# Output projection of a gated encoder layer as 2x2 block products: seven multiplications for eight, with the weight sums kept in DRAM

## The chip, the core and the metric

The kernel runs on one core of a Trainium2 chip. The core has TensorE (PE, matmuls, with its weight loads listed as PEld), VectorE (DVE), ScalarE (ACT), GpSimd (POOL) and SyncE (SP, which here only issues DMAs). SBUF is the working memory, PSUM takes the results of matmuls. The metric is the device time of one execution in microseconds.

## The reference

One encoder layer is applied to a prompt of 1024 tokens and a sample of 512 tokens, with the same weights. Three branches (pooling, self-attention, cross-attention) are projected to 1024 channels, gated and added; then comes the output projection that is changed here, a norm and the residual:

```
merged = jnp.zeros_like(x)
for n in range(N_BRANCH):
    merged = merged + gates[:, :, n] * (branches[n] @ w_branch[n])
y = rms_norm(merged @ w_out, ln_post)
return x + y
```

`w_out` is 1024 x 1024. Everything is float32.

## The kernel before

Each float32 matmul is done as three faster ones: an operand x is split into a high part (a copy rounded to the matmul's input type, made on ACT, L167) and a low part (x minus the high part, on DVE, L164), and `mm3` (L134) adds high x high, high x low and low x high in PSUM.

**Weights.** `weights` (L176) loads one tile of 128 x 1024 from DRAM into one of three raw buffers and splits it into `whi` and `wlo`. These have two buffers each (`NW`), so the split of a tile waits until PE is done with the tile before the last. Loads are issued by SP in its order. A raw buffer is free again when the low part is made.

**Input projection.** `products` (L323) already works on 2x2 blocks with seven products for the prompt's two token blocks. Beside it, small pieces of other work (`background`, L464) are run from a list `tasks`: the tails of keys, queries and pooling. One piece is taken at each product.

**Branches and merge.** The prompt is worked in two blocks of 512 tokens. `branches` (L1001) runs over three branches in the order 0, 2, 1 and over eight channel chunks d of 128. `merge` (L1051) multiplies one chunk; one weight tile serves two chunks, 24 matmuls of 512 columns. DVE applies the gate (L1064) and POOL adds to the accumulator (L1066). The accumulator is two tiles, `acc[0]` for channel chunks 0 to 3 and `acc[1]` for 4 to 7, each 128 x (4 x 512 tokens). In the last branch every second chunk is followed by a split of the two finished chunks (`split_pair`).

**Output projection.** `out_phase` (L1073) takes the split chunks as stationary operands, 128 tokens at a time, and the tiles of `w_out` as moving ones, in two column halves of 512. Each half runs over four weight tiles; a tile holds two chunks and serves 4 token tiles x 2 chunks x 3 = 24 matmuls. `evacuate` (L1093) reads each finished PSUM bank twice: DVE multiplies by the norm's row (`lnpost`) into `y`, ACT sums the squares. `finish` (L1081) makes the root mean square for two token tiles at a time (a sum on DVE, two small operations on POOL) and then scales and adds the residual on DVE (L1090), with low priority in the order. For the sample (`last`) there is a different ending.

The order of the instructions on each engine is made ahead of time by a scheduler from the code's order and the priorities (`AHEAD` for weight splits, `EVAC` for evacuations). On the chip each engine works through its own list in that order and waits for semaphores.

Of the kernel before, what the change touches and what calls it, by code (L numbers as in the profile page):

```python
# [14 lines left out]
AF = mybir.ActivationFunctionType  # L15
# [4 lines left out]
P = 128  # L20
D = 1024
# [41 lines left out]
def encoder_kernel(ctx: ExitStack, tc, wt, xs, xts, mt, cols, rows, rope, edge, ys):  # L63
# [112 lines left out]
    def weights(*key, pieces=1):  # L176

        raw = RAW()
        load(raw[:], wt[TILES[key]])
# [266 lines left out]
    def group(g):  # L446
# [53 lines left out]
        def gate_to_scratch(m, c0):  # L500
            def take(i, j, b, s):
                x = summed(b, s)
                o = HU()[:, :n] if s is None else s
# [144 lines left out]
    def pool_tail(c, ut, gate, T, out, wide, two_wide):  # L648
# [26 lines left out]
        for b in range(T // BLK):  # L675
# [324 lines left out]

    def branches(b, sc, merged):  # L1001

# [19 lines left out]
        def rest():  # L1022
            for i, (n, d) in enumerate(steps):
# [4 lines left out]
                if 2 <= d < 6 and n != order[-1]:  # L1028
                    chunk(order[order.index(n) + 1], d - 2)
                yield from merge(n, d, gates.pop(i), br, acc, merged if n == order[-1] else None)  # L1030

# [9 lines left out]
    def block(g, b, sc, last, merged=None):  # L1041
        bs = slice(b * BLK, (b + 1) * BLK)
        if merged is None:
            merged = []
            first, rest = branches(b, sc, merged)
            for f in first:
                f()
            yield from rest
        yield from out_phase(merged, xs[g][bs, :], ys[g][bs, :], last)

    def merge(n, d, sg, br, acc, merged):  # L1051

# [12 lines left out]
        if n > 0:  # L1065
            pool.tensor_tensor(at, at, sg, op=ALU.add)  # L1066
        if merged is not None and d % 2:
            merged.extend(split_pair(acc[d // 4][:, (d % 4 - 1) * BLK:(d % 4 + 1) * BLK]))
        yield

    held = []

    def out_phase(merged, src, dst, last):  # L1073
        y = [M(F32) for _ in range(2)]
# [6 lines left out]
        def finish(i):  # L1081
            ss = S(2)
            v.reduce_sum(ss[:], ssq[:, 2 * i:2 * i + 2, :2], axis=AX.X)
            rstd_of(ss[:])
            with tc.high_priority(-LATER):
                for j in range(2):
                    t = 2 * i + j
                    x = U()
                    load(x, src[t * P:(t + 1) * P, :])
                    v.scalar_tensor_tensor(x, yv[i][:, j], ss[:, j:j + 1], x, op0=ALU.mult, op1=ALU.add)  # L1090
                    nc.sync.dma_start(dst[t * P:(t + 1) * P, :], x)

# [5 lines left out]

        for half in range(1 if last else 2):
            o = [B(), B()] if half else [a[:, i * BLK:(i + 1) * BLK] for a in (A(),) for i in range(2)]  # L1100
            o += [a[:, i * BLK:(i + 1) * BLK] for a in (A(),) for i in range(2)]
            n = slice(half * BLK, half * BLK + BLK)
            for c in range(4):
                w = weights("half", half, c)
                for pair in ((0, 1), (2, 3)):
                    for kk in range(2):
                        k, s = c * 2 + kk, slice(kk * BLK, kk * BLK + BLK)
                        for t in pair:
                            ts = slice(t * P, (t + 1) * P)
                            mm3(o[t][:], (merged[k][0][:, ts], merged[k][1][:, ts]), w(s), k == 0, k == KC - 1)  # L1110
                    if c == 3:
                        for t in pair:
                            evacuate(t, n, o[t][:], half)
                    yield
        if last:
            av = A()[:].rearrange("p (t n) -> p t n", t=TT)
            for c in range(2):
                w = weights("out", 0, c)
                for kk in range(4):
                    k, s = c * 4 + kk, slice(kk * 256, kk * 256 + 256)  # L1120
                    for t in range(TT):
                        ts = slice(t * P, (t + 1) * P)
                        mm3(av[:, t], (merged[k][0][:, ts], merged[k][1][:, ts]), w(s),
                            k == 0 and t % 2 == 0, k == KC - 1 and t % 2 == 1)
                    yield
            for t in range(TT):
                evacuate(t, slice(512, 768), av[:, t], 1)
            yield from ending(merged, src, dst, yv, ssq, lnpost)
            return
        for i in range(2):  # L1130
            finish(i)

# [48 lines left out]
    bare = False  # L1181
    first, rest = branches(0, sc, merged)
    fill = chain(led(fill, len(pairs[1]) * 4, first), rest)
# [103 lines left out]
```

## Time and profile before

| | us |
|---|---|
| three runs | 1460.95, 1459.49, 1457.48 (median 1459.49) |
| the profiled execution | 1458.94 |
| its span, first to last instruction | 1456.7 |

One profile is taken of one execution. The parts read here are the page (busy times, and the span in 40 slices), the busy time of each engine by stretch, the groups of instructions, the chain of waits that ended last, and the timeline (start, duration, engine, line, output<-inputs, shape, and in brackets the idle time before it with what ended it). In a timeline row "x2" stands for two instructions in a row, with the time from the start of the first to the end of the second. Rows of an engine that follow each other closely overlap by some 0.1 us, so the distance of their starts is what one costs in a queue.

The stretches of the prompt's end are: branches of block 0 until 1187 us, its output projection until 1230, the branches of block 1 until 1296, its projection until 1340, then the sample.

### The profile page before, as it was taken

To read this page: it belongs to the slowest core of one execution; us is meant where nothing else is said; L and a number is where in the kernel's file an instruction comes from. 1 tells how busy PE (TensorE), PEld (TensorE's weight loads), DVE (VectorE), ACT (ScalarE), POOL (GpSimd) and SP (SyncE) were. 2 spreads that over 40 slices of the span, in tenths; PEclk is the share of its full clock that TensorE was granted. 3 is DMA by queue.
4 is the path that set the end of the run, shared out by engine and by line. 5 is a ranking of instruction groups with operands and counts; after the bars stand their busy time and mean duration, and the time that the engine had idled before them with its cause. 6 is when DMAs were issued, how large, how long until landed. Compare 5 with 4: busy or idle time off the path is not lost. (4 is left out here: it accounts for less than half of the span.)

```text
span 1456.7 us, 19518 instructions
## 1 busy us (share of the span) xinstructions
PE 1429.7 (98%) x7264; PEld 1198.0 (82%) x7264; DVE 969.6 (67%) x1211; ACT 712.1 (49%) x1085; POOL 276.0 (19%) x286
## 2 busy tenths in 40 slices
PE   6999999999999999999999999999999999999998
PEld 5878888888888888788888888888888888888887
DVE  6896586666557674565777666677676665765764
ACT  6454444544434545443666666677675233234232
POOL 1000020110000000210223322333333230240231
PEclk9999999999999999999999999999999999999999
DMA  8312243331422443244655665565447745945842
GB/s 288 118 64 98 80 131 115 114 132 61 132 93 69 153 145 123 87 163 148 240 204 192 222 216 189 209 209 172 148 159 266 270 127 180 333 166 184 329 137 86
DMA packets 95375, 238.65 MB, mean 164 GB/s; under 512 B 10672, under 2 KB 18992, under 8 KB 95280
## 3 DMA queue, kind: packets, MB, share of 16 engines
q1 hardware_dynamic: 86064, 203.84, 42.0%
q10 hardware_dynamic: 9216, 33.56, 5.9%
q8 instruction: 57, 0.93, 0.3%
q14 instruction: 38, 0.31, 0.1%
HBM read 151.38 MB, written 52.43 MB: 140 GB/s over the span
## 5 line engine op out<-in xcount | busy, mean ns | idle before, releaser
L128 PE MATMUL B<-med,whi 128*128 128x512 f32 x1576 | 492.0, 392 | 3.1 <-ACT med L440 1.3
L128 PE MATMUL A<-med,whi 128*128 128x512 f32 x1200 | 373.6, 392 | 1.4 <-ACT med L167 1.0
L128 PEld LDWEIGHTS B<-med,whi 128*128 128x128 f32 x1576 | 291.4, 188 | 62.7 <-ACT med L440 1.5
L167 ACT ACTIVATE whi<-raw 128x1024 fp32r<-128x1024 f32 (+1 forms) x169 | 167.4, 991 | 296.3 <-PE A L128 148.2
L128 PE MATMUL B<-med,wlo 128*128 128x512 f32 x788 | 308.0, 391 | 0.0
L164 DVE TENSOR_TENSOR wlo<-raw,whi 128x1024 fp32r<-128x1024 f32 (+1 forms) x169 | 212.1, 1255 | 139.3 <-ACT whi L167 137.7
L128 PEld LDWEIGHTS A<-med,whi 128*128 128x128 f32 x1200 | 223.1, 188 | 47.9 <-ACT med L167 1.2
L128 PE MATMUL A<-med,wlo 128*128 128x512 f32 x600 | 234.1, 390 | 0.1
L128 PEld LDWEIGHTS B<-med,wlo 128*128 128x128 f32 x788 | 147.9, 188 | 31.1
L189 POOL TENSOR_SCALAR s<-s 128x16 f32<-128x16 f32 (+3 forms) x17 | 7.5, 444 | 663.0 <-DVE s L582 324.0
L128 PEld LDWEIGHTS A<-med,wlo 128*128 128x128 f32 x600 | 112.6, 188 | 24.6 <-DVE wlo L164 0.8
L164 DVE TENSOR_TENSOR med<-A,med 128x1024 fp32r<-128x1024 f32 (+1 forms) x93 | 112.8, 1214 | 28.2 <-ACT med L167 26.6
L167 ACT ACTIVATE med<-A 128x1024 fp32r<-128x1024 f32 x92 | 94.2, 1025 | 68.5 <-PE A L132 68.1
L807 POOL TENSOR_SCALAR u<-u,s 128x1024 f32<-128x1024 f32 x64 | 72.3, 1129 | 212.3 <-DVE s L806 174.5
L803 DVE TENSOR_REDUCE s<-A 128x1 f32<-128x1024 f32 x64 | 77.8, 1215 | 36.8 <-PE A L128 31.8
L1066 POOL TENSOR_TENSOR med<-med,med 128x512 f32<-128x512 f32 x48 | 76.0, 1594 | 127.9 <-DVE med L1064 90.6
L128 PE MATMUL A<-whi,med 128*128 128x512 f32 (+1 forms) x352 | 98.3, 360 | 0.0
L805 ACT ACTIVATE u<-A,s 128x1024 f32<-128x1024 f32 x64 | 71.4, 1115 | 40.6 <-issue 23.4
L128 PE MATMUL A<-kt,med 128*128 128x512 f32 x320 | 87.8, 395 | 0.0
L167 ACT ACTIVATE whi<-sum 128x1024 fp32r<-128x1024 f32 x50 | 52.9, 1061 | 61.2 <-PE B L128 37.2
L164 DVE TENSOR_TENSOR med<-med,med 128x1024 fp32r<-128x1024 f32 (+1 forms) x50 | 55.6, 1120 | 32.7 <-ACT med L167 28.7
L164 DVE TENSOR_TENSOR wlo<-sum,whi 128x1024 fp32r<-128x1024 f32 x50 | 61.0, 1221 | 22.7 <-ACT whi L167 21.6
(197 smaller groups left out, 1899.3 us busy)
## 6 DMA issues: line engine op xcount, KB each, us to landing
raw<-wt SPq DMA_DIRECT2D x168, 512.0 KB, 3.7
u<-u ACTq DMA_DIRECT2D x64, 512.0 KB, 3.1
merge<-hu SPq DMA_DIRECT2D x72, 256.0 KB, 2.1
med<-merge SPq DMA_DIRECT2D x72, 256.0 KB, 5.7
med<-br SPq DMA_DIRECT2D x36, 256.0 KB, 5.3
q<-hu SPq DMA_DIRECT2D x24, 256.0 KB, 2.4
br<-hu SPq DMA_DIRECT2D x24, 256.0 KB, 2.8
med<-q SPq DMA_DIRECT2D x12, 512.0 KB, 4.8
```

Of the source, the lines that this page charges most:

```text
L128: pe.matmul(out, l, r, **k)
L164: v.tensor_tensor(out, x, hi.bitcast(F32), op=ALU.subtract)
L167: act.activation(hi, x, AF.Copy)
L189: pool.tensor_scalar(ss, ss, EPS, 1.0, op0=ALU.add, op1=ALU.mult)
L803: v.reduce_max(mx[:], a[:], axis=AX.X, negate=True)
L805: act.activation(p, a[:], AF.Exp, bias=mx[:], accum_out=sm[:])
L807: pool.tensor_scalar(p, p, rc[:], 1.0, op0=ALU.mult, op1=ALU.mult)
L1066: pool.tensor_tensor(at, at, sg, op=ALU.add)
```

## The change

The projection of a block becomes a product of 2x2 blocks: the tokens in two halves of 256, the channels in two halves of 512, the columns in two halves of 512. With quarters a11 to a22 of the merged block (`quarter`) and b11 to b22 of the weights, seven products are made in this order: a11 b11; a12 b21; s2 w2; s3 w3; s4 w4; s5 b22; a22 w6, where s3 = a21 + a22, s2 = s3 - a11, s4 = a11 - a21, s5 = a12 - s2. Each product has two weight tiles of 12 matmuls. The products are added up in three pairs of PSUM banks (X, Y, Z); three intermediate results are copied to SBUF by ACT (`keep`), and `put` adds them on DVE, takes the squares on ACT from SBUF, and multiplies by the norm's row on POOL.

The weight sums w2, w3, w4, w6 are made once by `out_weights`, a background task that is put on the list in the second pair of the first merge gate's projections, and are written to DRAM (`wsum`). Later they are loaded like any weight tile. The sample's projection is as before.

```diff
+    wsum = {i: scratch(f"wsum_{i}", [P, 2 * D]) for i in (2, 3, 4, 6)}
+    def out_weights():
+        for c in range(2):
+            b11, b12, b21, b22 = [U() for _ in range(4)]
+            for x, half, k in ((b11, 0, 0), (b12, 1, 0), (b21, 0, 2), (b22, 1, 2)):
+                load(x, wt[TILES["half", half, k + c]])
+            for _ in range(4):
+                yield
+            v.tensor_tensor(b12, b22, b12, op=ALU.subtract)
+            v.tensor_tensor(b11, b12, b11, op=ALU.add)
+            yield
+            v.tensor_tensor(b22, b22, b11, op=ALU.subtract)
+            v.tensor_tensor(b21, b21, b11, op=ALU.subtract)
+            yield
+            for i, x in ((4, b12), (2, b11), (3, b22), (6, b21)):
+                nc.sync.dma_start(wsum[i][:, c * D:(c + 1) * D], x)
+            yield
...
-        if merged is not None and d % 2:
-            merged.extend(split_pair(acc[d // 4][:, (d % 4 - 1) * BLK:(d % 4 + 1) * BLK]))
+        if parts:
+            parts(d, acc, merged)
...
+    def by_quarters(d, acc, merged):
+        if d == 3:
+            merged.append(quarter_parts(quarter(acc, 0, 0)))
+        elif d == 7:
+            merged.append([quarter(acc, i, j) for i in range(2) for j in range(2)])
...
+    def out_products(merged, src, dst):
...
+        def left(i):
+            if i == 1:
+                return quarter_parts(a12)
+            if i == 2:
+                total(3, a21, a22, ALU.add)
+                total(2, sums[3], a11, ALU.subtract)
+            elif i == 4:
+                total(4, a11, a21, ALU.subtract)
+            elif i == 5:
+                total(5, a12, sums[2], ALU.subtract)
+            return quarter_parts(a22 if i == 6 else sums[i])
...
+        def put(t, n, b, k):
+            ns = slice(n * BLK, (n + 1) * BLK)
+            x, junk = yv[t // 2][:, t % 2, ns], HU()
+            with tc.high_priority(EVAC):
+                if k is None:
+                    act.activation(x, b, AF.Copy)
+                else:
+                    v.tensor_tensor(x, b, kept.pop(k)[:], op=ALU.add)
+                act.activation(junk[:], x, AF.Square, scale=0.25 * D ** -0.5, accum_out=ssq[:, t, n:n + 1])
+            pool.tensor_tensor(x, x, lnpost[:, ns], op=ALU.mult)
...
+        for i in range(7):
+            lhs, bank = ahead, "XYXZXZX"[i]
...
+            for c in range(2):
+                w = right(i, c)
+                if c == 0 and i < 6:
+                    ahead = left(i + 1)
...
+                        mm3(b[u], (lhs[0][:, 2 * c + k, us], lhs[1][:, 2 * c + k, us]), w(ks),
+                            i in (0, 1, 3) and c == k == 0, c == k == 1, skip_group_check=True)
```

What stands in the lists of the engines is shown at two places. The first is VectorE's list in the first block's projection. Names are tile and instruction number; `wlo` is the low part of a weight tile, `med` from `med` or `u` the low part of a quarter or sum, `u` from two tiles a sum of quarters. Before, from the last weight tiles of the first column half on, with the two evacuations of L1096 between them:

```order
L164 TENSOR_TENSOR wlo_10840<-raw_10837,whi_10839 128x1024
L164 TENSOR_TENSOR wlo_10870<-raw_10867,whi_10869 128x1024
L164 TENSOR_TENSOR wlo_10915<-raw_10912,whi_10914 128x1024
L1096 TENSOR_TENSOR med_10769<-A_10775,u_10772 128x512 x2
L1096 TENSOR_TENSOR med_10770<-A_10776,u_10772 128x512
L164 TENSOR_TENSOR wlo_10945<-raw_10942,whi_10944 128x1024
```

Now, from the first weight tile of the third product (`wlo_10903`) to the first of the fourth (`wlo_10948`):

```order
L164 TENSOR_TENSOR wlo_10903<-raw_10900,whi_10902 128x1024
L1166 TENSOR_TENSOR med_10796<-B_10847,hu_10837 128x512
L1166 TENSOR_TENSOR med_10796<-B_10848,hu_10845 128x512
L164 TENSOR_TENSOR med_10906<-u_10855,med_10906 128x1024
L1134 TENSOR_TENSOR u_10996<-med_10239,u_10857 128x1024
L164 TENSOR_TENSOR wlo_10924<-raw_10921,whi_10923 128x1024
L164 TENSOR_TENSOR wlo_10948<-raw_10945,whi_10947 128x1024
```

Between two weight tiles of one product there stand now two additions, a low part and a sum, where one or no evacuation per weight tile stood before; each of these tiles serves half as many matmuls.

The second place is the end of the projection, on VectorE, where the first weight tile of the next block's branches (`wlo_11088` before, `wlo_11174` now) is made. Before it stood ahead of the whole end of the projection:

```order
L164 TENSOR_TENSOR wlo_11005<-raw_11002,whi_11004 128x1024
L164 TENSOR_TENSOR wlo_11088<-raw_11085,whi_11087 128x1024
L1096 TENSOR_TENSOR med_10769<-B_10909,u_10772 128x512
L1096 TENSOR_TENSOR med_10769<-B_10910,u_10772 128x512
L1083 TENSOR_REDUCE s_11044<-s_10771 128x2
L1090 SCALAR_TENSOR_TENSOR u_11048<-med_10769,s_11044,u_11048 128x1024
```

Now (`wlo_11107` is the last tile of the projection, L1211 the scaling with the residual):

```order
L164 TENSOR_TENSOR wlo_11107<-raw_11104,whi_11106 128x1024
L164 TENSOR_TENSOR med_11165<-med_11154,med_11165 128x2x512
L1204 TENSOR_REDUCE s_11130<-s_10798 128x2
L1211 SCALAR_TENSOR_TENSOR u_11134<-med_10796,s_11130,u_11134 128x1024
L1211 SCALAR_TENSOR_TENSOR u_11138<-med_10796,s_11130,u_11138 128x1024
L164 TENSOR_TENSOR wlo_11174<-raw_11171,whi_11173 128x1024
```

and POOL's list at the same place, on whose small operations (L189, L193) the scaling waits:

```order
L1168 TENSOR_TENSOR med_10796<-med_10796,u_10799 128x512 x2
L1168 TENSOR_TENSOR med_10797<-med_10797,u_10799 128x512 x2
L1168 TENSOR_TENSOR med_10796<-med_10796,u_10799 128x512 x2
L189 TENSOR_SCALAR s_11130<-s_11130 128x2
L193 TENSOR_TENSOR s_11130<-s_11130,mhalf 128x2
L1168 TENSOR_TENSOR med_10797<-med_10797,u_10799 128x512 x2
```

The reduction and the two scalings have moved ahead of that weight tile, and they stand behind three pairs of multiplications on POOL that were not there.

More of the change, by code (lines that the diff above doesn't have):

```diff
@@ L178, in weights @@
         raw = RAW()
-        load(raw[:], wt[TILES[key]])
+        load(raw[:], key[0] if len(key) == 1 else wt[TILES[key]])
         hi, lo = WT()
@@ L999, in cross, with branches @@
         return [(ahead, scores, turn, values, None, c, 3410) for c in range(NXH)]
-    def branches(b, sc, merged):
+    def branches(b, sc, merged, parts):
         bs = slice(b * BLK, (b + 1) * BLK)
@@ L1029, in rest @@
                     chunk(order[order.index(n) + 1], d - 2)
-                yield from merge(n, d, gates.pop(i), br, acc, merged if n == order[-1] else None)
+                yield from merge(n, d, gates.pop(i), br, acc, merged, parts if n == order[-1] else None)
         return [partial(chunk, order[0], c) for c in range(4)] + [partial(gate, i) for i in range(2)], rest()
@@ L1044, in block @@
             merged = []
-            first, rest = branches(b, sc, merged)
+            first, rest = branches(b, sc, merged, by_chunks if last else by_quarters)
             for f in first:
@@ L1048, in block, with merge @@
             yield from rest
-        yield from out_phase(merged, xs[g][bs, :], ys[g][bs, :], last)
-    def merge(n, d, sg, br, acc, merged):
+        yield from (out_phase if last else out_products)(merged, xs[g][bs, :], ys[g][bs, :])
+    def merge(n, d, sg, br, acc, merged, parts):
         if not acc:
@@ L1066, in merge, with by_chunks, quarter, quarter_parts @@
             pool.tensor_tensor(at, at, sg, op=ALU.add)
-        if merged is not None and d % 2:
-            merged.extend(split_pair(acc[d // 4][:, (d % 4 - 1) * BLK:(d % 4 + 1) * BLK]))
-        yield
+        if parts:
+            parts(d, acc, merged)
+        yield
+    def by_chunks(d, acc, merged):
+        if d % 2:
+            merged.extend(split_pair(acc[d // 4][:, (d % 4 - 1) * BLK:(d % 4 + 1) * BLK]))
+    def by_quarters(d, acc, merged):
[3 more added lines that the diff above has]
+            merged.append([quarter(acc, i, j) for i in range(2) for j in range(2)])
+    def quarter(acc, i, j):
+        return acc[j][:].rearrange("p (c n) -> p c n", c=4)[:, :, i * 256:(i + 1) * 256]
+    def quarter_parts(x):
+        t = M()
+        hi, lo = [t[:, i * D:(i + 1) * D].rearrange("p (c n) -> p c n", c=4) for i in range(2)]
+        split(hi, lo, x)
+        return hi, lo
     held = []
-    def out_phase(merged, src, dst, last):
+    def out_tiles():
         y = [M(F32) for _ in range(2)]
@@ L1079, in out_phase @@
         v.tensor_scalar_mul(lnpost, lnpost, 0.25)
[L1081 to L1091, printed above, removed]
+        return yv, ssq, lnpost
@@ new lines, in finish, with out_phase @@
+    def finish(i, yv, ssq, src, dst):
+        ss = S(2)
+        v.reduce_sum(ss[:], ssq[:, 2 * i:2 * i + 2, :2], axis=AX.X)
+        rstd_of(ss[:])
+        with tc.high_priority(-LATER):
+            for j in range(2):
+                t = 2 * i + j
+                x = U()
+                load(x, src[t * P:(t + 1) * P, :])
+                v.scalar_tensor_tensor(x, yv[i][:, j], ss[:, j:j + 1], x, op0=ALU.mult, op1=ALU.add)
+                nc.sync.dma_start(dst[t * P:(t + 1) * P, :], x)
+    def out_phase(merged, src, dst):
+        yv, ssq, lnpost = out_tiles()
@@ L1115, in out_phase @@
[L1115 to L1121, printed above, removed]
-                        ts = slice(t * P, (t + 1) * P)
[L1123 to L1129, printed above, removed]
@@ L1130, in out_phase @@
-        for i in range(2):
-            finish(i)
+        o = [a[:, i * BLK:(i + 1) * BLK] for a in (A(), A()) for i in range(2)]
+        for c in range(4):
+            w = weights("half", 0, c)
+            for pair in ((0, 1), (2, 3)):
+                for kk in range(2):
+                    k, s = c * 2 + kk, slice(kk * BLK, kk * BLK + BLK)
+                    for t in pair:
+                        ts = slice(t * P, (t + 1) * P)
+                        mm3(o[t][:], (merged[k][0][:, ts], merged[k][1][:, ts]), w(s), k == 0, k == KC - 1)
+                if c == 3:
+                    for t in pair:
+                        evacuate(t, slice(0, BLK), o[t][:], 0)
+                yield
@@ new lines, in out_phase @@
+        av = A()[:].rearrange("p (t n) -> p t n", t=TT)
+        for c in range(2):
+            w = weights("out", 0, c)
+            for kk in range(4):
+                k, s = c * 4 + kk, slice(kk * 256, kk * 256 + 256)
+                for t in range(TT):
+                    ts = slice(t * P, (t + 1) * P)
+                    mm3(av[:, t], (merged[k][0][:, ts], merged[k][1][:, ts]), w(s),
+                        k == 0 and t % 2 == 0, k == KC - 1 and t % 2 == 1)
+                yield
+        for t in range(TT):
+            evacuate(t, slice(512, 768), av[:, t], 1)
@@ L1133, in ending @@
+        yield from ending(merged, src, dst, yv, ssq, lnpost)
     def ending(merged, src, dst, yv, ssq, lnpost):
@@ L1181, in encoder_kernel @@
     bare = False
-    first, rest = branches(0, sc, merged)
+    first, rest = branches(0, sc, merged, by_quarters)
     fill = chain(led(fill, len(pairs[1]) * 4, first), rest)
```

55 lines of the change are left out of this document (39 added, 16 removed).

## The prediction

> **What bounds the kernel now.** I read the page first: the share of each engine and the clock that TensorE was granted.
>
> ```profile
> span 1456.7 us, 19518 instructions
> PE 1429.7 (98%) x7264; PEld 1198.0 (82%) x7264; DVE 969.6 (67%) x1211; ACT 712.1 (49%) x1085; POOL 276.0 (19%) x286
> PEclk9999999999999999999999999999999999999999
> ```
>
> PE is busy 98% of the span at nearly its full clock, so a matmul taken away is time taken away, as long as PE is still what the stage waits for. Next I read the busy time by stretch (us of PE, PEld, DVE, ACT, POOL, then clock and DMA): the branches of the first prompt block, its output projection, the branches of the second, its output projection.
>
> ```profile
> 1117.00:1186.00 69.00, 69.00 (x306) 57.07 (x305) 46.41 (x48) 18.94 (x19) 21.08 (x15) 1.00 0.70 238
> 1186.00:1230.00 44.00, 44.00 (x196) 36.44 (x195) 20.34 (x21) 16.02 (x24) 4.08 (x3) 1.00 0.48 149
> 1230.00:1296.00 66.00, 66.00 (x293) 54.66 (x292) 47.54 (x49) 20.05 (x22) 24.04 (x18) 1.00 0.77 275
> 1296.00:1340.00 44.00, 43.95 (x195) 36.05 (x194) 20.45 (x21) 16.23 (x24) 4.65 (x5) 1.00 0.48 155
> ```
>
> In the two output projections PE never waits. DVE is busy 20 of 44 us and POOL 4. That is the room the change has to live in.
>
> **What is removed.** The chain of waits gives the pace of TensorE there (start, us, what):
>
> ```profile
> 1146.67 2.72 PE A L128 x12
> ```
>
> Twelve 512-column matmuls take 2.72 us, 0.227 each. A block has 2 halves x 8 chunks x 4 token tiles x 3 = 192 of them, 43.5 us. Seven products of 2 tiles x 4 chunks x 3 are 168, 38.1 us. **24 fewer, 5.44 us a block, 10.9 us in all**, if nothing waits.
>
> **What is added in the projection.** A weight tile (load, high part on ACT, low part on DVE) served 24 matmuls, 5.44 us; now it serves 12, 2.72 us. There are 14 tiles a block instead of 8, 6 more splits of quarter sums, 4 sums, 6 additions from PSUM, 6 copies, and 8 multiplications on POOL. All weight tiles share two buffers, so tile t+2 cannot begin before PE has left tile t. What these take, from the timeline at the end of the first projection (start, duration, form, idle before):
>
> ```profile
> 1209.31 1.06 ACT L167 ACTIVATE whi<-raw 128x1024 fp32r<-128x1024 f32 x1
> 1210.28 0.59 ACT L1097 ACTIVATE hu<-A 128x512 f32<-128x512 f32 x1
> 1210.76 0.19 ACT L1097 ACTIVATION_READ_ACCUMULATOR hu<-A 128x1 f32 x1
> 1230.11 0.19 POOL L189 TENSOR_SCALAR s<-s 128x2 f32<-128x2 f32 x1 [36.94 <-DVE s L1083]
> 1230.38 0.71 POOL L193 TENSOR_TENSOR s<-s,mhalf 128x2 f32<-128x2 f32 x1
> 1231.13 1.28 DVE L1090 SCALAR_TENSOR_TENSOR u<-med,s,u 128x1024 f32<-128x1024 f32 x1 [1.11 <-POOL s L193]
> 1232.93 1.21 DVE L164 TENSOR_TENSOR wlo<-raw,whi 128x1024 fp32r<-128x1024 f32 x1
> 1234.06 0.68 DVE L1096 TENSOR_TENSOR med<-A,u 128x512 f32<-128x512 f32 x1
> 1234.66 0.67 DVE L1064 SCALAR_TENSOR_TENSOR med<-med,B 128x512 f32<-128x512 f32 x1
> ```
>
> Starts in a row give the cost in a queue: DVE 1.14 us for 1024 columns (1232.93 to 1234.06) and 0.60 for 512, ACT 0.97 for 1024 and 0.60 for a square with its sum. The chain of a tile is 0.97 + 1.14 and hand-overs, some 2.3 us of 2.72; any other instruction between delays PE. ACT has (14 + 6) x 0.97 + 8 x 0.60 + 8 copies x 0.50 = 28 us to do in 38, so it is not the bound.
>
> The new POOL multiplications have the form of L1066's additions (128x512, both inputs in SBUF). These rows, one stretch of DVE and POOL, show what they do to DVE:
>
> ```profile
> 1182.81 0.68 DVE L1064 SCALAR_TENSOR_TENSOR med<-med,A 128x512 f32<-128x512 f32 x1
> 1183.03 3.52 POOL L1066 TENSOR_TENSOR med<-med,med 128x512 f32<-128x512 f32 x2 [3.09 <-DVE med L1064]
> 1183.40 2.00 DVE L164 TENSOR_TENSOR wlo<-raw,whi 128x1024 fp32r<-128x1024 f32 x1
> 1155.63 1.29 POOL L1066 TENSOR_TENSOR med<-med,med 128x512 f32<-128x512 f32 x1 [1.43 <-DVE med L1064]
> 1155.73 2.27 DVE L164 TENSOR_TENSOR wlo<-raw,whi 128x1024 fp32r<-128x1024 f32 x1 [0.18 <-ACT whi L167]
> ```
>
> At 1155.73 the low part starts 0.10 us after a POOL addition of 1.29, and takes 2.27 = 1.19 of waiting + 1.08 of work. At 1183.40 it waits for the first addition, and the second one waits for it (3.52 for the two instead of 2.58). So they exclude each other and take turns; a POOL operation costs a waiting DVE 1.25 us. The instruction at 1182.81 reads PSUM and SBUF, overlaps the same addition, and keeps its 0.68. The new sums, the splits of the quarters and the closing scale-and-add read two SBUF tiles as the low part does, so I price them like it, by the nearest row. [...]
>
> **The sum for one block.** I lay the four queues of the order end to end with these prices. Time 0 is where the last branch matmul ends; tiles are numbered 1 to 14, two a product.
> - The last branch sum leaves POOL at 1.98. Tile 2's low part waits for it, until 3.11: PE waits 0.26. Sum, low part of a12, tile 3: 6.53, PE waits 0.70. Two more sums and tile 4: 9.95, PE waits 0.47. Low part, tile 5: 12.23, in time.
> - Product 3: two additions from PSUM 13.45, a low part 14.59, POOL 15.84, a sum 16.98, POOL 18.23, tile 6 19.37. PE left tile 5 at 15.0 and has four matmuls that need only high parts: it waits 3.51 in all. Tile 8 waits for ACT's copies after product 3: 0.13. Tiles 9 to 11 come in time.
> - Before product 6's second tile: two additions 33.03, a low part 34.17, POOL 35.42, the scaling of the next block's norm row (1024 columns, one input) 36.03, POOL 37.28, tile 12 38.42: PE waits 2.61. Tile 14: 0.40. PE ends product 7 at 46.2, not 38.1.
> - The end: tile 14 43.81, POOL 45.06, a low part 46.20, the root on POOL (0.19 + 0.71) 47.42, POOL 48.67, scale-and-add 49.87, POOL 51.12, scale-and-add 52.32, and only then the low part of the next branch's first weights, 53.46. PE waits 0.49 + 1.16 + 4.60 = 6.25.
>
> Waits of 0.26 + 0.70 + 0.47 + 3.51 + 0.13 + 2.61 + 0.40 + 6.25 = 14.3 us, less 5.44 saved: **+8.9 us a block**. Unknown is the lock on operations that the rows do not show: none of it gives -0.4, one turn lost each time (DVE always first) +5.0. I take the alternation because the rows at 1183 show it. Both blocks end in a branch stage of the same code, so twice +8.9 = 17.8.
>
> **Making the sums.** It adds 8 loads of 512 KB, 8 DVE operations of 1024 (9.1 us) and 8 stores on SP's queue, in the projection of the prompt's merge gates.
>
> ```profile
> 283.00:344.00 61.00, 61.00 (x284) 50.46 (x283) 35.99 (x50) 27.55 (x40) 4.88 (x5) 1.00 0.33 108
> 309.11 0.69 DVE L164 TENSOR_TENSOR wlo<-raw,whi 128x512 fp32r<-128x512 f32 x1 [2.59 <-ACT whi L167]
> 311.82 0.69 DVE L442 TENSOR_TENSOR hu<-A,hu 128x512 f32<-128x512 f32 x1 [2.02 <-PE A L128]
> 314.90 0.69 DVE L442 TENSOR_TENSOR hu<-B,hu 128x512 f32<-128x512 f32 x1 [2.39 <-PE B L128]
> raw<-wt SPq DMA_DIRECT2D x168, 512.0 KB, 3.7
> ```
>
> DVE is idle 25 of 61 us there, in holes of 2 to 2.6 us, and POOL hardly works. Below nothing is excluded, as no matmul goes. Above: the weights' loads stand on SP behind stores that wait for DVE; one such load late by its 3.7 us, in each of the two passes, is 7.4 us. I take 0.3, near the end with the cover shown. Two fewer splits of the merged block before each projection lie in DVE's idle time and save nothing.
>
> The profiled execution took 1458.94 us (span 1456.7 and 2.2 around it), 0.55 under the median of 1459.49. 1458.9 + 17.8 + 0.3 = **1477**.
>
> **The rivals.**
> - TensorE's clock falls after the long waits (0.23). At the start of the trace there is one such wait, and the clock beside it:
>
> ```profile
> 26.40 0.80 PE L128 MATMUL A<-mh,whi 128*128 128x512 f32 x1 [2.88 <-ACT whi L167]
> 24.00:34.00 10.00, 7.56 (x24) 5.35 (x24) 6.61 (x8) 6.37 (x6) 2.52 (x2) 0.66 0.66 227
> ```
>
> After 2.88 us of idle PE the mean clock of ten us is 0.66: at half speed that is (1 - 0.66) x 2 x 10 = 6.8 us, and 3.4 us of work lost. My longest wait is 4.6, the next 2.8. One drop a block gives 1484, two 1491. Against it: PE had been busy only in pieces before that one. [...]
> - DVE gets the port whenever it asks (0.13): +5.0 a block, 1469. The waits before the end fall from 8.1 to 5.6 us, those at the end from 6.3 to 4.9.
> - No lock (0.09): the same queues without turns leave 0.10 + 0.47 + 1.01 + 0.13 + 0.67 + 2.65 = 5.0 us of waits against 5.44 saved, 1458. The rows at 1155 and 1183 speak against it.
> - Faster (0.05): the projection stays PE-bound, as the stretch 1186 to 1230 is now, and the whole 10.9 us come through: 1448. It decides at what stands between a tile's high and low part: with up to 0.4 us between, 2.72 holds. For it: DVE is idle 24 of 44 us now. Against: 14 + 6 + 4 operations at 1.14 and 6 at 0.60 are 31 us, and 8 at 1.25 on POOL make 41, in 38.1.
> - That the 24 matmuls do not go: the order has them gone, so no chance is given.
>
> **How the numbers follow.** My own case has 0.50, and with the clock's fall 0.73. From 1464, which takes in DVE first with a little to spare, to 1491, two drops a block, stands about 0.85. The upper end of the sums' cost lies inside it. A measurement of this kernel tells 0.2% (2.9 us) from no change. Faster: 0.05; within: the case without lock, 0.09; slower: 0.86.
>
> **What would show it.** Right: PE idle in the two projections, mostly put down to L164's low parts, 14 us a block, with one wait of 3 to 5 us at the first weights of the next branches; DVE's low parts with a mean above 1.5 us in the projection, POOL's multiplications near 2; no idle PE between 250 and 350. Wrong: the multiplications at 1.29 and the low parts at 1.22 in the same stretch (no lock); PE waiting for loads of the sums from DRAM; the granted clock below 0.99 after the projections (the clock rival).

## The result, and the profile after

The changed kernel takes 1479.43 us (median of 4 runs, 1477.91 to 1481.37), the kernel before in the same comparison 1460.07. The ratio is 1.0135, 95% interval 1.012 to 1.015: some 19 us slower, where 1477 was forecast. The profiled execution took 1479.42 us, its span 1477.6, 20.9 more than the span before.

The page's first lines and its row of the granted clock:

```profile
span 1477.6 us, 19576 instructions
PE 1433.7 (97%) x7216; PEld 1192.9 (81%) x7216; DVE 1013.1 (69%) x1241; ACT 737.6 (50%) x1119; POOL 313.9 (21%) x302
PEclk9999999999999999999999999999999998998999
```

PE executes 48 matmuls fewer, and is still busy 4 us longer than before: some of them ran slowly, and part of the waiting is counted as busy (below). The clock row shows where they ran slowly, in two slices near the end. Busy time by stretch (us of PE, PEld, DVE, ACT, POOL, then clock and DMA), for branches, projection, branches, projection:

```profile
1117.00:1187.00 70.00, 70.00 (x311) 57.99 (x310) 45.83 (x47) 18.43 (x19) 21.93 (x16) 1.00 0.65 215
1187.00:1245.00 58.00, 49.46 (x187) 36.70 (x186) 45.00 (x41) 32.91 (x47) 24.08 (x13) 0.91 0.66 229
1245.00:1306.00 61.00, 61.00 (x271) 50.51 (x270) 40.82 (x40) 16.54 (x16) 22.11 (x15) 1.00 0.69 239
1306.00:1366.00 60.00, 51.14 (x193) 38.13 (x192) 45.61 (x42) 32.96 (x47) 22.65 (x13) 0.91 0.66 223
```

In both projections PE is now idle, and its mean clock is 0.91. Nothing like this stands in the branches. What PE waits for in the first projection (total, times, longest):

```profile
PE B L128 <- DVE wlo L164: 5.6, 5, 3.5
PE B L128 <- ACT whi L167: 1.9, 3, 0.8
PE A L128 <- ACT whi L167: 0.7, 1, 0.7
PE A L128 <- DVE wlo L164: 0.3, 1, 0.3
```

These are waits for split weights, high or low part, as forecast. The view counts the time in which PE did nothing at all, 8.5 us here. What the waits cost I take from the starts of the matmuls: each 512-column matmul has 0.227 us before the next one starts; what is above that is a wait, except steps of 0.40 to 0.46 us, which are matmuls at half clock (a single step of that length, with no fall in the record of the clock, is a short wait).

| us a block | forecast | first block | second block |
|---|---|---|---|
| tiles 2 to 4 | 1.43 | 1.79 | 1.78 |
| product 3 | 3.51 | 1.07 | 1.01 |
| tiles 8 and 10 | 0.13 | 0.83 | 0.87 |
| products 6 and 7 | 3.01 | 2.84 | 3.88 |
| end of product 7 and the next branch's first weights | 6.25 | 6.04 | 5.13 |
| half clock | 0 | 3.4 | 4.0 |
| matmuls saved | -5.44 | -5.44 | -5.44 |
| sum | +8.9 | +10.5 | +11.2 |

The blocks in the two traces differ by 10.5 and 10.9 us (the second block of the kernel before has 0.3 us of waits itself).

The half clock follows the two long waits of each block. Stretches of the first one, cut where the clock changes, with the 3.41 us ahead of each fall (same columns):

```profile
1220.77:1224.18 3.41, 1.38 (x6) 0.51 (x5) 2.84 (x3) 1.06 (x1) 1.53 (x2) 1.00 1.00 328
1224.18:1227.59 3.41, 3.41 (x9) 2.64 (x10) 2.05 (x3) 1.44 (x2) 0.00 (x0) 0.50 1.05 402
1227.59:1231.00 3.41, 3.41 (x17) 2.72 (x16) 2.96 (x4) 2.96 (x6) 1.48 (x2) 1.00 0.73 280
1234.42:1237.83 3.41, 0.99 (x4) 0.23 (x2) 3.41 (x3) 1.89 (x4) 3.41 (x2) 1.00 0.38 154
1237.83:1244.66 6.83, 4.91 (x12) 3.90 (x13) 4.59 (x5) 0.00 (x0) 1.68 (x3) 0.50 0.50 157
```

Between 1224.18 and 1227.59 PE is busy all the time with 9 matmuls, where the next 3.41 us have 17.

**DVE and POOL.** The timeline around product 3 (start, duration, form), rows of DVE and then POOL's first two multiplications by the norm row:

```profile
1200.59 1.21 DVE L164 TENSOR_TENSOR med<-u,med 128x1024 fp32r<-128x1024 f32 x1
1201.72 1.21 DVE L1134 TENSOR_TENSOR u<-med,u 128x1024 f32<-128x1024 f32 x1
1202.85 2.35 DVE L164 TENSOR_TENSOR wlo<-raw,whi 128x1024 fp32r<-128x1024 f32 x2
1205.12 2.35 DVE L164 TENSOR_TENSOR med<-u,med 128x1024 fp32r<-128x1024 f32 x2
1200.90 9.96 POOL L1168 TENSOR_TENSOR med<-med,u 128x512 f32<-128x512 f32 x2 [11.60 <-ACT hu L1167]
```

They do exclude each other, but here they don't take turns: DVE starts an instruction every 1.14 us as if POOL weren't there, and POOL's two need 9.96 us instead of 2.5 (one of this form alone took 1.28 at 1188.02). The first alone takes 7.74, until DVE pauses at 1207.5. This is so at product 3 of both blocks. It is not so everywhere: at the end of the projection they do take turns (below). In the projection DVE's low parts take 1.32 us in the mean and POOL's multiplications 2.64 (grouped by form, 1187 to 1233 and 1187 to 1240):

```profile
L164 DVE TENSOR_TENSOR wlo<-raw,whi 128x1024 fp32r<-128x1024 f32 x13 | 16.9, 1315 | 5.6 <-ACT whi L167 5.6
L1168 POOL TENSOR_TENSOR med<-med,u 128x512 f32<-128x512 f32 x8 | 21.0, 2639 | 27.2 <-ACT hu L1167 27.2
```

**Product 6.** Here DVE stood still ahead of a low part. The timeline of the first and of the second projection:

```profile
1221.34 1.51 DVE L1123 TENSOR_SCALAR u<-u 128x1024 f32<-128x1024 f32 x1 [1.42 <-DMA u<-rows]
1222.78 2.35 DVE L164 TENSOR_TENSOR wlo<-raw,whi 128x1024 fp32r<-128x1024 f32 x2
1342.47 0.69 DVE L1123 TENSOR_SCALAR u<-u 128x1024 f32<-128x1024 f32 x1 [3.21 <-DMA u<-rows]
1343.08 2.35 DVE L164 TENSOR_TENSOR wlo<-raw,whi 128x1024 fp32r<-128x1024 f32 x2
```

L1123 scales the norm row for the *next* block. The prediction priced it at its own 0.6 us; DVE waited 1.4 and 3.2 us there for its load, with two low parts behind it.

**The end** went as laid out: two closing scale-and-adds, then the first low part of the next branch, with POOL's last multiplications in between. Each of these pairs takes longer than twice its work (1.14 us on DVE, 1.25 on POOL): DVE and POOL wait for one another by turns, though DVE's instructions stand in a row here too.

```profile
1233.99 3.50 DVE L1211 SCALAR_TENSOR_TENSOR u<-med,s,u 128x1024 f32<-128x1024 f32 x2 [2.19 <-POOL s L193]
1237.42 3.41 DVE L164 TENSOR_TENSOR wlo<-raw,whi 128x1024 fp32r<-128x1024 f32 x2
1234.35 4.27 POOL L1168 TENSOR_TENSOR med<-med,u 128x512 f32<-128x512 f32 x2 [0.39 <-ACT hu L1167]
```

**The sums of the weights** cost nothing: between 250 and 350 us PE is busy without a pause in both kernels, DVE 7.7 us more. The kernel before:

```profile
250.00:350.00 100.00, 100.00 (x467) 82.53 (x466) 61.85 (x82) 44.94 (x64) 10.91 (x10) 1.00 0.32 105
```

The changed kernel:

```profile
250.00:350.00 100.00, 100.00 (x468) 82.54 (x467) 69.51 (x90) 45.23 (x64) 10.91 (x10) 1.00 0.54 188
```

### The profile page after: what moved, and what is told of

Same layout as the page of the kernel before. It is cut to its first block, busy times and chain, and to the rows that moved or that the text cites. A ratio compares the mean times of both kernels' runs of the same rounds, so it can differ in the third digit from the quotient of the medians.

```text
span 1477.6 us, 19576 instructions
## 1 busy us (share of the span) xinstructions
PE 1433.7 (97%) x7216; PEld 1192.9 (81%) x7216; DVE 1013.1 (69%) x1241; ACT 737.6 (50%) x1119; POOL 313.9 (21%) x302
## 5 line engine op out<-in xcount | busy, mean ns | idle before, releaser
L167 ACT ACTIVATE whi<-raw 128x1024 fp32r<-128x1024 f32 (+1 forms) x181 | 180.0, 995 | 306.0 <-PE A L128 170.0
L164 DVE TENSOR_TENSOR wlo<-raw,whi 128x1024 fp32r<-128x1024 f32 (+1 forms) x181 | 231.8, 1284 | 116.0 <-ACT whi L167 113.9
L189 POOL TENSOR_SCALAR s<-s 128x16 f32<-128x16 f32 (+3 forms) x17 | 9.3, 546 | 581.4 <-DVE s L584 323.1
L1088 POOL TENSOR_TENSOR med<-med,med 128x512 f32<-128x512 f32 x48 | 71.2, 1492 | 135.9 <-DVE med L1086 135.9
L128 PE MATMUL A<-whi,med 128*128 128x512 f32 (+1 forms) x320 | 91.5, 365 | 1.8 <-ACT whi L167 1.8
L128 PE MATMUL B<-med,vt 128*128 128x256 f32 x512 | 74.7, 287 | 1.3 <-DVE med L164 1.2
```

Of the source, the lines that this page charges most:

```text
L128: pe.matmul(out, l, r, **k)
L164: v.tensor_tensor(out, x, hi.bitcast(F32), op=ALU.subtract)
L167: act.activation(hi, x, AF.Copy)
L189: pool.tensor_scalar(ss, ss, EPS, 1.0, op0=ALU.add, op1=ALU.mult)
```

## The experiments

Theory W, formed on the way: a tile that serves 12 matmuls has 2.72 us, its buffer comes free only two tiles before, and so *whatever* stands beside its two splits is a wait. Further theories stand in the expectations: P (of e5, that POOL's multiplications cause the waits at product 6) and D (of e9, that a load is late because its buffer comes free late). The rivals: the lock by turns of the prediction (L), the load of the norm row in DVE's queue (N), and, for the size of the effects, whether the clock falls with the waits (C).

The medians of whole runs hold some 3 us that come from elsewhere (in the profile of e1 the first 400 matmuls alone, some 100 us, end 2.7 us later, with a fall of the clock at 90 us, where its edit changes nothing). So the effect is read from the two blocks in each profile. "Block 1" is the time from the 5,731st matmul, in the first block's branches, to the 6,241st, in the next block's; "block 2" from there to the 6,731st. In the kernels with the old projection 24 and 48 are added to the counts. Each ratio is to runs of the kernel before that were made together with the kernel in question; their median was between 1459.2 and 1460.4 us.

| kernel | median us | ratio to before, interval | block 1 | block 2 | half clock, both |
|---|---|---|---|---|---|
| before | 1459.5 | | 121.1 | 116.9 | 0.2 |
| changed | 1479.4 | 1.0135, 1.012 to 1.015 | 131.6 | 127.8 | 7.4 |
| e1 no scaling on DVE | 1479.2 | 1.0121, 1.0102 to 1.0141 | 130.3 | 125.3 | 4.8 |
| e2 closing later | 1467.3 | 1.0041, 1.0027 to 1.0056 | 123.8 | 121.9 | 3.1 |
| e3 no norm multiplications | 1466.8 | 1.0043, 1.0028 to 1.0058 | 126.1 | 120.1 | 1.2 |
| e4 = e1 and e2 | 1464.2 | 1.0025, 1.0013 to 1.0038 | 123.9 | 119.0 | 0.5 |
| e5 = e4, norm row at the close | 1463.1 | 1.0021, 1.0011 to 1.0032 | 123.2 | 119.1 | 0 |
| e6 = changed, 3 weight buffers | 1465.9 | 1.0043, 1.0028 to 1.0059 | 127.8 | 121.6 | 4.0 |
| e7 = e5, 3 weight buffers | 1451.8 | 0.9937, 0.9914 to 0.9960 | 119.9 | 113.7 | 1.6 |
| e8 = before, buffers of e7 | 1456.2 | 0.9969, 0.9958 to 0.9979 | 121.0 | 116.5 | 0 |
| e9 = e7, 4 loaded tiles | 1443.6 | 0.9886, 0.9868 to 0.9904 | 116.1 | 111.3 | 0.2 |
| e10 = before, buffers of e9 | 1454.0 | 0.9958, 0.9944 to 0.9972 | 121.0 | 116.5 | 0 |
| e11 = changed, buffers of e9 | 1458.9 | 0.9988, 0.9976 to 1.0000 | 123.8 | 117.1 | 3.6 |
| e12 = e9, norm on POOL again | 1446.1 | 0.9907, 0.9893 to 0.9922 | 117.5 | 112.9 | 0 |

**e1, no scaling of the norm row on DVE**

```diff
-    def rstd_of(ss):
+    def rstd_of(ss, by=1.0):
...
-        pool.tensor_scalar(ss, ss, EPS, 1.0, op0=ALU.add, op1=ALU.mult)
+        pool.tensor_scalar(ss, ss, EPS, by, op0=ALU.add, op1=ALU.mult)
...
-        v.tensor_scalar_mul(lnpost, lnpost, 0.25)
...
-        rstd_of(ss[:])
+        rstd_of(ss[:], 16.0)
```

The sample's ending gets the same factor.

> The scaling of the norm row by 0.25 (L1123, one DVE instruction a block, which stands in DVE's queue in the projection and waits there for the row's load) is taken out; the factor goes into the root on POOL instead (16 times the mean square under the root). The same is computed. Theory N (the trace of the change): the waits at product 6, 2.5 us in the first projection and 3.3 in the second, come from DVE standing at L1123 until the row has landed (1.42 and 3.21 us of idle DVE), and TensorE runs at half clock for some 4 us behind them (another 2.0 to 2.6 us). Both go: PE loses at most 0.6 us there, no half clock in the middle of the projections, 4 to 5 us less a block, 1470 in all. Theory L (the prediction's lock by turns): the wait at product 6 is DVE and POOL taking turns at the norm multiplications; one DVE instruction less saves 0.6 us a block, 1478, and the half clock stays.

The blocks became 1.3 and 2.4 us shorter, not 4 to 5, and the median doesn't show it. DVE no longer waits at L1123. The same low parts now stand behind POOL (timeline of e1, DVE and POOL at product 6):

```profile
1224.28 3.87 DVE L164 TENSOR_TENSOR wlo<-raw,whi 128x1024 fp32r<-128x1024 f32 x2 [0.61 <-ACT whi L167]
1222.61 4.45 POOL L1167 TENSOR_TENSOR med<-med,u 128x512 f32<-128x512 f32 x2 [8.00 <-ACT hu L1166]
```

Two low parts take 3.87 us instead of 2.35, PE waits 0.5 and 1.2 us in product 7, where it had waited in product 6, and in the first block the clock falls twice again, in the second once. In the changed kernel the standstill at L1123 had covered POOL's multiplications. N is right about the standstill and wrong about what it costs: under it lay the next wait.

**e2, the closing scale-and-adds later**

```diff
-        for i in range(2):
-            finish(i, yv, ssq, src, dst)
+        waiting.extend(partial(finish, i, yv, ssq, src, dst) for i in range(2))
...
+        if d == 1 and waiting:
+            eps = S(1)
+            pool.tensor_scalar(eps[:], at[:, :1], 0.0, EPS, op0=ALU.mult, op1=ALU.add)
+            while waiting:
+                waiting.pop(0)(eps[:])
```

The second piece stands in `merge`, behind the gate of chunk 1; `finish` hands `eps`, which depends on that chunk, to the root.

> The two roots and four scale-and-adds that close a block (L1204 to L1212) are made to depend on the second chunk of the next branch stage, so that they stand in DVE's queue behind the first three weight tiles of that stage. The same is computed. At the end of a projection PE now waits 5.9 us in all, of which 3.5 and 2.75 us in one piece for the low part that stands behind two scale-and-adds. All theories: that one piece falls below 1 us, some 3 us less a block. Theory C (the clock falls behind a long wait): the half clock behind it (2.4 us of lost time in the first block, 1.7 in the second) goes as well, 5 us a block in all, 1469. Without C: 3 us a block, 1473, and TensorE still shows a granted clock of 0.5 there. If the scale-and-adds take PE's time elsewhere in the branch stage (DVE is busy 47 of 66 us there), idle PE appears within the 15 us behind the projection and the gain is under 2 us a block.

7.8 and 5.9 us less a block, 1467.3 (expected 5 a block and 1469). The waits are 4.6 and 4.7 us shorter, the half clock 3.2 and 1.2. The wait of 3.5 us at the end is gone, and behind it the clock stays at 1.00 where the changed kernel had 0.50. A window of e2 over the first projection's end and the next branches:

```profile
1230.00:1260.00 30.00, 29.02 (x126) 23.08 (x125) 23.75 (x25) 11.86 (x17) 9.43 (x9) 1.00 0.85 288
```

The gain is some twice the 3 us that stand for it without C. In the first block part of it is luck: the half clock at product 6 stayed away too, though the wait there was nearly as long as before (why, the last section shows). The rest of the branch stage has no new idle PE.

**e3, without the multiplications by the norm row**

```diff
-            pool.tensor_tensor(x, x, lnpost[:, ns], op=ALU.mult)
```

> The eight multiplications by the norm row on POOL (L1168) are left out, so the output of the prompt lacks that factor. Theory L (lock by turns, as in the prediction): the waits fall from 14.3 to 5.0 us a block by the same sum without turns, 1479.4 - 2 x 9.3 = 1461. Theory N (DVE, once it runs back to back, keeps the port and POOL waits; the waits before the end come from the chain of splits, from L1123 and from the clock): in the projection nothing changes, only the end gains, because the root on POOL comes some 2 us earlier and the first low part of the branches isn't held 1.2 us: 2 to 3 us a block, 1474.

5.5 and 7.7 us less a block, between the two theories (2 to 3 and 9.3). The waits at tiles 2 to 4 and at product 3 stay as they were to 0.05 us: POOL has no part in those, against L. Of the waits, what went is some 0.1 us at tile 8, some behind L1123, and above all the end, where the root comes earlier and the two low parts take 2.35 us instead of 3.41: 2.9 and 2.5 us are left there, and the forecast's walk without turns had 2.65. So at the end L was right. The half clock that followed is 2.2 and 4.0 us shorter.

**e4, e1 and e2 together**

> Both edits of the first two together: no scaling of the norm row on DVE, and the closing scale-and-adds behind the first weights of the next stage. The same is computed. Theory N with C: the gains add up, 9 + 10 us, 1479.4 - 19 = 1460, where what is left of the waits (0.6 + 0.6 + 0.4 + 1.0 + 0.5 + 0.2 in the products, 1.7 at the first matmuls of the branches, 5 us a block) uses up the 5.44 us saved, and the granted clock is 1.00 from 1100 to the end. Theory L: 1479.4 - 1 - 6 = 1472.

1464.2, 4 us above what N with C expected. The clock does not fall any more. Against e2 alone, block 1 is the same and block 2 is 2.9 shorter, where half clock went. Each block is still 2 to 3 us longer than before.

**e5, the norm row at the close** (against e4)

```diff
-            pool.tensor_tensor(x, x, lnpost[:, ns], op=ALU.mult)
...
-                v.scalar_tensor_tensor(x, yv[i][:, j], ss[:, j:j + 1], x, op0=ALU.mult, op1=ALU.add)
+                y = yv[i][:, j]
+                v.scalar_tensor_tensor(y, y, ss[:, j:j + 1], lnpost, op0=ALU.mult, op1=ALU.mult)
+                v.tensor_tensor(x, x, y, op=ALU.add)
```

> Both edits of e4, and the eight multiplications by the norm row leave POOL: the closing scale-and-add becomes two DVE instructions of 1024 columns in the next branch stage, (value x root) x norm row, then plus the input. The same is computed; POOL does nothing in the projections. Theory P (in e1 and e4 the wait at product 6 came back because the low parts there stand behind POOL's multiplications, 3.86 us for two instead of 2.3): PE's waits at products 6 and 7 (0.9, 0.5 and 1.2 us in e4's first block, 0.7, 0.2 and 1.2 in its second) fall to the 0.7 or so of the hand-over from ACT, 1 to 2 us less a block, 1461; block 1 from 123.9 us to some 122.3. Rival (two weight buffers set the pace there, and POOL only fills DVE's pauses): under 0.5 us a block, 1464. The four added DVE instructions of 1.14 us a block lie in the branch stage; if they aren't hidden, idle PE appears in the 20 us behind the projection.

0.8 us less in block 1, 0.1 more in block 2, 1463.1: nearer to the rival. With POOL out of the projection and L1123 gone, PE still waits (waits of PE in e5's first projection):

```profile
PE A L128 <- ACT whi L167: 1.4, 2, 1.0
PE B L128 <- ACT whi L167: 1.1, 2, 0.6
PE A L128 <- DVE wlo L164: 0.9, 2, 0.5
PE B L128 <- DVE wlo L164: 0.7, 3, 0.4
```

High and low parts come late in nine small pieces, which neither N nor L explains. By the starts of the matmuls the waits before the end of product 7 are 6.4 and 6.5 us a block, about as many as in the changed kernel (6.5 and 7.5).

**e6, three buffers for split weights**

```diff
-NU, NM, NHU, NRAW, NW = 7, 14, 9, 3, 2
+NU, NM, NHU, NRAW, NW = 6, 14, 7, 3, 3
```

`NW` counts the buffers for split weight tiles, `NRAW` those for tiles as loaded; `NU` and `NHU` are the 4-KB and 2-KB buffers.

> The changed kernel with three buffers for split weight tiles instead of two; the room comes from one of the seven 4-KB and two of the nine 2-KB buffers. The same is computed. Theory W (a tile that serves 12 matmuls, 2.72 us, leaves no room for a second DVE instruction between its parts as long as its buffer comes free only two tiles before): the waits at tiles 2 to 4 (1.7 us), product 3 (1.0) and tile 8 (0.5) go, and those at product 6 with the half clock behind them, since L1123 and POOL then have another 2.72 us: 3 + 4 to 5 us a block, while the end stays (5.9 us and its half clock): 1479.4 - 15 = 1464. Rival (DVE has too much to do in the projection, some 30 of 45 us with POOL's turns, and a third buffer only moves the wait): the same waits later, 1475 or more.

3.8 and 6.1 us less a block. All waits in products 1 to 7 are gone but one of 0.25 us, though POOL's multiplications and the sums are where they were (L1123 itself moved out of the projection with the smaller pool; that alone is not it, since e4, without L1123, still has 7.2 and 6.8 us of waits there). What is left stands at the next branch's first weights, and is longer than it was:

```profile
PE B L128 <- DVE wlo L164: 5.8, 2, 5.5
PE B L128 <- ACT whi L167: 2.6, 1, 2.6
```

**e7 and its control e8**

> e5 with the three weight buffers of e6. The same is computed. Theories P and W together: no wait in the projection is left but those at the first matmuls of the branches (1.7 us a block in the change, from ACT), so a block saves 5.44 - 1.7 to 5.44 - 0: 119 to 117.5 us for the first block where the kernel before has 121.1, the granted clock stays at 1.00, and the time is 1459.8 - 7 to - 11, 1449 to 1453. If a third buffer doesn't help: as e5.

> The kernel before with the three weight buffers and the smaller pools of e6 and e7, as their control. The same is computed. All theories: PE never waited in the projections, so nothing is to be gained there; within 3 us of 1459.8. If it is faster by more than that, part of what e6 and e7 gain is the buffers elsewhere and not the products; if it is slower, the smaller pools cost something in the other stages.

e7 takes 1451.8, as expected, though the clock still falls once, and is faster than the kernel before by 0.4 to 0.9%. Its control is faster as well, by 0.2 to 0.4% and more than the 3 us allowed for, with projections as long as before (121.0 and 116.5): the buffers gain some 4 us, nearly all in stages that the change doesn't touch. By the blocks, the products save 1.1 and 2.8 us. One wait is left in each. In the first projection it is this one:

```profile
PE B L128 <- ACT whi L167: 2.2, 1, 2.2
```

In the timeline, the split that PE waits for, and the issue of its load:

```profile
1226.05 1.06 ACT L167 ACTIVATE whi<-raw 128x1024 fp32r<-128x1024 f32 x1 [0.99 <-DMA raw<-wt]
1219.97 0.33 SPq L141 DMA_DIRECT2D raw<-wt  x1
```

The load is issued at 1219.97, when a raw buffer comes free, and lands 6 us later.

**e9 and its control e10** (e9 against e7)

```diff
-NU, NM, NHU, NRAW, NW = 6, 14, 7, 3, 3
+NU, NM, NHU, NRAW, NW = 6, 14, 5, 4, 3
```

> e7 with four buffers for weights as loaded instead of three; the room is two more of the 2-KB buffers (five are left). The same is computed. What is left of the waits in e7 is one piece a block, 2.24 and 1.75 us at the first weights of the next branches: the high part there waits for a load that was issued 6 us before and whose issue waited for a free buffer, and some 1.4 us at half clock follow in the first block. Theory D (the load is late because its buffer comes free late): the pieces fall below 0.5 us, 1.5 to 3.5 us less a block, 1446 to 1449. Rival (the load takes 6 us because the transfers of that stretch run at nearly all the DMA engines can move, whenever it is issued), or the 2-KB buffers are now too few: 1451 or more, with the wait where it was or a new one behind the copies that products keep.

> The kernel before with the buffers of e9, as its control. The same is computed. All theories: PE doesn't wait in the projections, so those stay; within 2 us of the control with three weight buffers, 1456, unless the few 2-KB buffers cost something in the attention, which would show as idle PE before 1110 us.

1443.6, below what was expected: theory D. In the projection and behind it PE is idle for 0.02 us of 50 (windows of e9):

```profile
1184.00:1224.00 40.00, 40.00 (x178) 32.88 (x177) 33.92 (x32) 28.61 (x41) 1.44 (x2) 1.00 0.69 240
1224.00:1234.00 10.00, 9.98 (x44) 7.97 (x43) 7.78 (x11) 4.64 (x8) 4.06 (x5) 1.00 0.79 270
```

Against the control the blocks are 4.9 and 5.2 us shorter, of 5.44 that the matmuls are worth, and the medians differ by 10.4 us of 10.9. So nearly the whole saving is there when nothing waits. DVE is busy 34 of those 40 us, and in e12 below, with POOL's multiplications back, 37: the amount of work on DVE and POOL, which spoke against the forecast's rival "faster", doesn't forbid it.

**e11, the changed kernel with these buffers and nothing else**

> The changed kernel with the buffers of e9 (three for split weights, four for loaded ones) and none of the other edits. The same is computed. Theory W (the buffers set the waits in the products, the queue of the closing scale-and-adds those at the end): no wait is left in the products, and one of some 5 us with the half clock behind it stays at the first weights of the next branches, some 7 us a block: 1443.6 + 14 = 1458, about the kernel before. Rival (the edits of e4 and e5 carried the gain of e9, the buffers little): waits come back at products 3 and 6, 1465 or more.

1458.9, as W expects: the buffers alone give back 20 us, 18.5 of them in the two blocks, and the kernel is level with the one before (and 0.3% behind the control e10, whose blocks are 2.7 and 0.6 us shorter). Waits of PE in e11's first projection:

```profile
PE B L128 <- DVE wlo L164: 3.5, 2, 3.3
PE B L128 <- DVE med L164: 0.8, 1, 0.8
```

The 3.3 us are the end of the projection, with 2.2 us at half clock behind them.

**e12, e9 with the norm multiplications on POOL**

> e9 with the eight multiplications by the norm row back on POOL in the projection (no scaling of the row on DVE, closing scale-and-adds late). The same is computed. Theory W: with one more weight tile ahead, 2.72 us, a low part that stands 1.2 or 1.6 us behind POOL is still in time; PE waits under 0.5 us in the products, 1443 to 1446. Theory L (the lock is a cost of its own on the path): 1 to 3 us of waits a block at products 3 and 6, 1446 to 1450, with the low parts there above 1.5 us in the mean.

1446.1, 1.4 and 1.6 us more a block than e9. The waits (first projection):

```profile
PE B L128 <- DVE med L164: 0.8, 1, 0.8
PE B L128 <- DVE wlo L164: 0.2, 1, 0.2
```

Products 3 and 6 are in time, as W says; one small wait stands at a weight's low part in the products, one at the low part of the next branch's operand. The time itself lies where the two theories meet. DVE and POOL take turns in this run, at product 3 too, where DVE's instructions follow each other without a pause (timeline, DVE and POOL):

```profile
1198.05 1.21 DVE L164 TENSOR_TENSOR wlo<-raw,whi 128x1024 fp32r<-128x1024 f32 x1
1199.18 2.31 DVE L164 TENSOR_TENSOR med<-u,med 128x1024 fp32r<-128x1024 f32 x1
1198.10 2.31 POOL L1172 TENSOR_TENSOR med<-med,u 128x512 f32<-128x512 f32 x1 [1.06 <-ACT hu L1171]
```

So L's turns are there (the second low part takes 2.31 us, the first 1.21), and one more tile ahead covers them at products 3 and 6. With the rings of e9, POOL's multiplications in the projection cost 2.5 us more of the whole time than the same work at the close.

## Why the prediction came out as it did

- **The matmuls saved** were right: 48 are gone, and e9 shows nearly their full worth, 4.9 and 5.2 of 5.44 us a block.
- **The chain of a tile** was right as a place and as a reason, and priced too low. With two buffers, high part, low part and anything else do not fit into 2.72 us. The walk without turns had 2.4 us of waits before the end of product 7 (0.10 + 0.47 + 1.01 + 0.13 + 0.67). e5, with no work of POOL and no L1123 in the projection, has 6.4 and 6.5. All six kernels of the new product with two buffers have 6.4 to 7.6 there, whatever stands beside the splits, and the five with three have 0.2 to 0.8. This is what turns the change from a gain into a loss: e5 is 0.2% slower than the kernel before, and e9, which is e5 with more buffers, 1.1% faster (its control e10, the kernel before with these buffers, 0.4%). Which hand-over makes the 4 us that the walk lacks has not been taken apart; 2.5 of the 4.1 us that PE idles in e5's first projection and right behind it are waits for the high part, and the walk had nearly all of it on the low part.
- **The step that failed is the lock by turns at product 3.** The walk let POOL in twice there. In the trace DVE ran six instructions through and POOL waited; the wait is 1.07 and 1.01 us instead of 3.51, the walk without turns had 1.01, and e3 shows that POOL has no part in it. The turns themselves were not wrong: at the end of the projection they came, and 6.25 us became 6.04 and 5.13, where the rival "DVE gets the port whenever it asks" had 4.9 and e3 without POOL has 2.9 and 2.5. What decides between the two is open, and no run shows a port: the word in that rival's name, and in theory N of e3, was an assumption of the author's.
- **Product 6** had the right size (3.0 forecast with tile 14, 2.8 and 3.9 measured) for a wrong reason. The walk put POOL there. In the trace DVE stood at L1123, whose load the walk took as landed; e1 then uncovered POOL's share. But e5, with neither, still has 2.8 in both blocks, and only the third buffer of e6 removed it.
- **The clock** was kept out of the likeliest case, as a rival with one or two falls a block at 3.4 us each. There are two falls a block, worth 1.4 to 2.6 us each, 3.4 and 4.0 us a block. In e2 and e4 they go with the waits.
- So that 1477 came near 1479.4 is luck: three errors nearly cancel. Before the end of product 7 the chain is some 4 us a block above the walk's 2.4; of the 5.7 us of turns that the walk put there, at most some 1 us came; and there are 3.4 to 4.0 us at half clock instead of none. What happened is a mixture of the forecast's case, the rival with DVE first and the rival on the clock. Of the signs that were named, the place of the waits and the long wait at the next branch's first weights came; DVE's low parts took 1.32 us and not above 1.5, and POOL's multiplications 2.64 in the mean, 1.9 without the one of 7.74; and the clock below 0.99, the sign of the rival, came too.
- **The sums of the weights** at 0.3 us: nothing is to be seen, as expected.

## What to carry to other kernels

Fewer matmuls per loaded tile is a change of the load and split rate before it is a change of the matmul count: here, with half the matmuls to a tile, the rings of loaded and of split tiles each had to be a tile deeper. When a wait is removed and the time stays, look for the next wait that had lain under it, and test the depth of the ring before the instructions that fill it. A price for a wait on PE must include the slow matmuls that can follow it (3.4 and 4.0 us a block in the changed kernel), and a kernel with other buffers needs a control with the old code.

## What the runs showed of the hardware

- GpSimd and VectorE instructions, each with two SBUF inputs, waited for one another. In the 14 traces a GpSimd instruction came 52 times while VectorE ran one of 1024 columns with the next right behind it. 43 times GpSimd had the next turn, and VectorE's next instruction took some 2.3 us instead of 1.21 (in the changed kernel 2.28 to 2.31 us, four times at the ends of the projections). 9 times VectorE went on: 8 of them are product 3 in the changed kernel, e1, e2 and e4, where GpSimd's 1.25 us took 7.74 (both blocks of the changed kernel; the two instructions together 9.96 there, 9.97 in e1, 9.96 in e4) and VectorE was not slowed (1.21 us an instruction); in the changed kernel five VectorE instructions that started later went ahead of GpSimd's there. The order of VectorE's instructions there is the same in all four kernels; what decides is open.
- TensorE's clock fell to 0.50 without one long idle stretch. In each trace its changes stand on one grid of 3.41 us, which lies differently to the start of the span in each run (in the kernel before a step starts at 25.28 us, in the changed one at 26.10), and half clock lasts one to three steps of it (3.41, 6.83 or 10.24 us). Behind the first 60 us of the 14 traces, all 16 falls in the course of the work came right behind a step with 1.60 to 3.41 us of idle PE; the four of the changed kernel had 2.03, 2.42, 2.28 and 2.75. Steps at full clock with up to 1.68 us idle passed without a fall (1.67 at 86.71 us of the kernel before, 1.68 at 1469.94 of the changed one), and in the course of the work none with more. In e3 the 1.60 us were made of pieces of at most 0.85 us. So in these traces about half a step was enough, with both outcomes between 1.60 and 1.68 us, and it counted on which side of a boundary the idle time lay: the wait at product 6 made 2.03 us of idle PE in one step of the changed kernel (1220.77 to 1224.18, above), and in e2 nearly the same wait is cut in two, 0.75 and 1.28 us, with the clock at 1.00 in both steps:

```profile
1221.40:1224.81 3.41, 2.66 (x11) 1.44 (x9) 1.32 (x2) 2.20 (x4) 2.95 (x2) 1.00 0.96 308
1224.81:1228.22 3.41, 2.13 (x9) 1.79 (x10) 3.03 (x4) 1.05 (x1) 0.00 (x0) 1.00 1.05 402
```
